# Corner merges of six triangular inverses in seven shared runs, with paired modulation tiles

## The chip, the cores and the metric

The kernel runs on one core of a Trainium2 chip. The metric is the device time of one execution in microseconds (us). TensorE (PE in the profile) has two parts there: PE for the matmuls and PEld for the loads of their stationary operands. VectorE is DVE, ScalarE is ACT, GpSimd is POOL, and SP issues nearly all DMAs from one queue.

## The reference

Two layers of a diffusion backbone run over 128 context tokens and 256 latent tokens, 384 in all, which the kernel handles as three token tiles of 128. A layer computes a modulated RMSNorm, one wide input projection, three mixers (A: windowed attention, B: latent attention, C: a gated delta rule in both directions), a gated merge of the three branches, an output projection and a squared-ReLU MLP. The parts that the change touches are these:

```python
def adaln(cond, w, bias):                       # the modulation vectors
    return (jax.nn.silu(cond) @ w + bias)[:, None, :]
...
    a_mat = jnp.where(strict, jnp.einsum('bhnid,bhnjd->bhnij', kb, kc) * decay, 0.0)
    eye = jnp.eye(C_CHUNK, dtype=f32)
    t_mat = lax.linalg.triangular_solve(eye + a_mat, jnp.broadcast_to(eye, a_mat.shape),
                                        left_side=True, lower=True, unit_diagonal=True)
    u = t_mat @ (vc * bc[..., None])
...
def rmsnorm(x, g):
    xf = x.astype(jnp.float32)
    y = xf * lax.rsqrt(jnp.mean(xf * xf, axis=-1, keepdims=True) + EPS)
    return (y * g.astype(jnp.float32)).astype(x.dtype)
```

The inverse of the unit triangular 128x128 matrix is wanted for 3 token tiles, 2 directions and 4 heads.

## The kernel before, in words

Nearly all of TensorE's work is the dense projections. A weight tile of 128x1024 (512 KB) is loaded into a `raw` buffer (three of them), ACT rounds it into `whi` (L147) and DVE subtracts to get `wlo` (L148), and `mm3` (L151 to L153) forms each product from three matmuls of 384 columns.

Every engine runs its instructions in an order that is fixed when the program is built. Within a phase of a layer a piece of work belongs to a stream, and the order is made by priority: `chain` first, then `fill`. The chain of branch C is a long sequence of small steps; while it waits for DVE or ACT, the matmuls of `merge` (the dense gates and branch projections) and of `beside` fill TensorE.

The inverse is made in two stages. First 32x32 diagonal blocks of all 24 matrices are inverted together on DVE (31 steps, L847 and L849), which gives `Xc` and `XcT` in a packed form. Then, for each of the six pairs of token tile `n` and direction `d`, a loop (L865 to L897) merges blocks: it spreads the packed blocks into full 128x128 tiles `X0` and `X0T` (two DVE products with a block-diagonal mask, L870), cuts the blocks that couple 32-neighbours out of the matrix `M` with `mask5` (`M5`, L865), and then runs five groups of four matmuls (one for each head) with an evacuation between each two: W = M5 X0T (128x128), a product for the transposed 64-block (64 columns of the array), W X0 (128x128), and two 64x64x64 products that fill the last corner. A float32 matmul stands in the profile as two records. ACT evacuates with L878 and L893, DVE with L886, L888 and L897. One merge starts after the other in program order; all matmuls go through the helper `mm` (L156).

`rows` (L188) turns a column of per-token factors into a row repeated on all partitions: three bf16 `pieces` (L177, four DVE instructions) of the factor are each multiplied with an identity, accumulating. It is used for every RMSNorm and for the output gates of branch C.

`ada` (L277) computes modulation rounds 1 and 2 of layer 0: each step loads one 512 KB half tile of `w_ada` and issues four matmuls that write 32 partitions each (groups `g`). `merge(2, more, (1, 1))` calls one step in each of its eight iterations, using the `raw` buffers, and `merge(1, more, (3, 3))` three in each, using three buffers `araw`. `ada_sums` (L294) computes layer 1's modulation on DVE during layer 0's MLP: one step (two DVE instructions, L313) in each of the 32 iterations of the first MLP product, two in each of the 32 of the second, 96 in all.

## Time and profile before

| | |
|---|---|
| median of 3 runs | 1564.96 us (1561.77 to 1565.35) |
| the profiled execution | 1564.52 us, of which 1562.7 us lie between its first and last instruction (the span) |
| busy share of the span | PE 97%, PEld 89%, DVE 65%, ACT 49%, POOL 1% |
| mean granted TensorE clock | 0.993 of full speed |
| DMA | 212.82 MB, 136 GB/s in the mean |

A matmul's recorded duration covers its passage through the array, so two matmuls that follow each other overlap in the record. What one costs is read from the distance between starts. The numbers of layer 0's stages repeat in layer 1 some 779 us later.

### The profile page before, as it was taken

What the parts mean: (1) busy time and instruction counts of PE and PEld (TensorE: products, weight loads), DVE (VectorE), ACT (ScalarE), POOL (GpSimd) and SP (SyncE); (2) the same over time, 40 slices, a digit from 0 to 9 for tenths busy, and PEclk for the clock granted to TensorE, in tenths of its full rate; (3) what the DMA queues carried; (4) which work ended last, traced back from release to release, by engine and by line L of the source; (5) the groups of instructions that cost most, each with busy time, mean ns of one, the idle gap of its engine ahead of it and who ended that gap; (6) DMA issues with size and microseconds to landing.
All of it is one profiled execution on the core that took longest, in us unless ns stands there. A gap on an engine that the chain in (4) does not pass through costs nothing.

```text
span 1562.7 us, 25131 instructions
## 1 busy us (share of the span) xinstructions
PE 1521.6 (97%) x9652; PEld 1396.2 (89%) x9652; DVE 1013.9 (65%) x2187; ACT 771.8 (49%) x1522; POOL 12.9 (1%) x34
## 2 busy tenths in 40 slices
PE   5999999999999999999999999999999999999998
PEld 3898788987888999999988987889888999999997
DVE  4667896475435877789986778955655565553332
ACT  3466633346524666643344676334465446664222
POOL 0000100000000000000000001000000000000000
PEclk9999999999999999999998999999999999999999
DMA  9532131143488555578763331311424434433332
GB/s 315 162 103 88 48 95 48 59 145 105 141 291 279 160 175 176 176 236 259 252 187 98 95 95 47 96 49 58 129 61 135 130 118 126 126 122 129 128 122 81
DMA packets 80857, 212.82 MB, mean 136 GB/s; under 512 B 8801, under 2 KB 24545, under 8 KB 80609
## 3 DMA queue, kind: packets, MB, share of 16 engines
q1 hardware_dynamic: 80736, 211.21, 42.7%
q8 instruction: 76, 1.25, 0.3%
q14 instruction: 45, 0.36, 0.1%
HBM read 204.59 MB, written 4.75 MB: 134 GB/s over the span
## 4 chain that ended last, share of the span: by engine, by line
PE 86%; DVE 8%; DMA 4%; ACT 1%; issue 1%; SPq 0%; DVEq 0%; ACTq 0%
PE g L151 22%; PE g L153 22%; PE g L152 22%; PE c L156 9%; PE f L156 3%; DMA araw<-in_w_ada_dram 2%; PE o L156 2%; PE f L443 2%; DVE wlo L148 2%; PE g L156 1%; DVE h L847 1%; DVE blk L849 1%; DMA mraw<-in_w_ada_dram 1%; PE c L151 1%; PE c L153 1%
## 5 line engine op out<-in xcount | busy, mean ns | idle before, releaser
L147 ACT CAST whi<-raw 128x1024 fp32r<-128x1024 f32 x268 | 280.8, 1048 | 463.6 <-PE g L152 408.0
L153 PE MATMUL g<-hh,wlo 128*128 128x384 f32 (+1 forms) x1440 | 495.2, 345 | 2.8 <-DVE wlo L148 2.7
L151 PE MATMUL g<-hh,whi 128*128 128x384 f32 (+1 forms) x1440 | 494.8, 345 | 3.1 <-ACT hh L229 1.5
L152 PE MATMUL g<-hl,whi 128*128 128x384 f32 (+1 forms) x1440 | 493.6, 344 | 1.3 <-DVE hl L230 1.0
L148 DVE TENSOR_TENSOR wlo<-raw,whi 128x1024 fp32r<-128x1024 f32 x268 | 326.0, 1217 | 168.5 <-PE g L153 123.1
L151 PEld LDWEIGHTS g<-hh,whi 128*128 128x128 f32 x1440 | 272.2, 189 | 14.9 <-issue 6.3
L153 PEld LDWEIGHTS g<-hh,wlo 128*128 128x128 f32 x1440 | 272.5, 189 | 12.4 <-DVE wlo L148 6.0
L152 PEld LDWEIGHTS g<-hl,whi 128*128 128x128 f32 x1440 | 272.2, 189 | 8.1 <-issue 2.7
L151 PE MATMUL g<-fh,whi 128*128 128x384 f32 x512 | 172.9, 338 | 0.0
L152 PE MATMUL g<-fl,whi 128*128 128x384 f32 x512 | 172.1, 336 | 0.0
L153 PE MATMUL g<-fh,wlo 128*128 128x384 f32 x512 | 172.1, 336 | 0.0
L313 DVE SCALAR_TENSOR_TENSOR aacc<-araw,cs,aacc 128x512 f32<-128x512 f32 x168 | 116.5, 747 | 11.0 <-DMA araw<-in_w_ada_dram 6.9
L151 PEld LDWEIGHTS g<-fh,whi 128*128 128x128 f32 x512 | 96.2, 188 | 1.6 <-issue 1.6
L152 PEld LDWEIGHTS g<-fl,whi 128*128 128x128 f32 x512 | 96.3, 188 | 0.0
L153 PEld LDWEIGHTS g<-fh,wlo 128*128 128x128 f32 x512 | 96.3, 188 | 0.0
L156 PE MATMUL c<-g,g 128*128 128x128 f32 (+1 forms) x608 | 77.5, 274 | 3.6 <-DVE g L870 3.1
L156 PEld LDWEIGHTS c<-g,g 128*128 128x128 f32 (+1 forms) x608 | 69.9, 182 | 11.3 <-ACT g L878 4.0
L151 PE MATMUL g<-brh,whi 128*128 128x384 f32 x192 | 66.4, 346 | 0.4 <-ACT whi L147 0.4
L152 PE MATMUL g<-brl,whi 128*128 128x384 f32 x192 | 65.7, 342 | 0.0
L153 PE MATMUL g<-brh,wlo 128*128 128x384 f32 x192 | 65.6, 342 | 0.0
L424 ACT ACTIVATE at_p<-at_p,at_nm 128x384 f32<-128x384 f32 (+1 forms) x96 | 51.8, 541 | 24.7 <-DVE at_nm L421 23.9
L148 DVE TENSOR_TENSOR fl<-fa,fh 128x384 fp32r<-128x384 f32 x64 | 35.6, 556 | 41.9 <-ACT fh L147 41.9
(312 smaller groups left out, 1862.3 us busy)
## 6 DMA issues: line engine op xcount, KB each, us to landing
raw<-in_w_ff_dram SPq DMA_DIRECT2D x128, 512.0 KB, 3.6
raw<-in_w_in_dram SPq DMA_DIRECT2D x102, 512.0 KB, 3.6
araw<-in_w_ada_dram SPq DMA_DIRECT2D x96, 256.0 KB, 3.4
raw<-in_w_branch_dram SPq DMA_DIRECT2D x24, 512.0 KB, 3.6
araw<-in_w_ada_dram SPq DMA_DIRECT2D x24, 512.0 KB, 6.4
raw<-in_w_out_dram SPq DMA_DIRECT2D x16, 512.0 KB, 4.3
mraw<-in_w_ada_dram SPq DMA_DIRECT2D x8, 512.0 KB, 9.2
mraw<-in_w_ada_dram SPq DMA_DIRECT2D x16, 256.0 KB, 7.6
```

The source lines that it names most:

```text
L147: S.copy(hi, src)
L148: V.tensor_tensor(out=lo, in0=src, in1=hi.bitcast(F32), op=ALU.subtract)
L151: PE.matmul(ps, lhsT=wh, rhs=rh, start=start, stop=False)
L152: PE.matmul(ps, lhsT=wh, rhs=rl, start=False, stop=False)
L153: PE.matmul(ps, lhsT=wl, rhs=rh, start=False, stop=stop)
L156: return PE.matmul(ps, lhsT=lhsT, rhs=rhs, start=start, stop=stop)
L313: V.scalar_tensor_tensor(out=acc[:, s, :], in0=raw, scalar=cs[:, k, s:s + 1], in1=acc[:, s, :], op0=ALU.mult, op1=ALU.add)
L424: S.activation(sm[:, :nk], sm[:, :nk], AF.Exp, bias=nm[:, u:u + 1], scale=-1.0, accum_out=den[:, u:u + 1])
L443: PE.transpose(pt[:, j * P:(j + 1) * P], ps_[half, n][:, c * P:(c + 1) * P], ident)
L847: V.tensor_tensor(out=tmp, in0=Cb[:, j + 1:, j:j + 1].to_broadcast([P, r, w]), in1=X[:, j:j + 1, :w].to_broadcast([P, r, w]), op=ALU.mult)
L849: V.tensor_tensor(out=X[:, j + 1:, :w], in0=X[:, j + 1:, :w], in1=tmp, op=ALU.subtract)
```

## The change

The edits are these.

- The six merges are no longer done one after the other. Their products are cut into 64x64x64 pieces, 28 for each (n, d) in place of 20 matmuls, and issued in seven `run`s that mix token tiles and steps. Within a run the pieces alternate between the upper and the lower half of the contraction partitions (`r`), each half with a PSUM bank of its own (`pair`, `twin`). `spread` writes only two 32-blocks per row, so it has 256 columns instead of 512. Evacuations work on 64 partitions. `M5` and the copy `M2` are gone: GpSimd zeroes the 32x32 diagonal blocks of `M` in place instead, and the result is written back into `M`.
- `rows` transposes the float32 column, broadcast to 128 columns, in place of three bf16 matmuls; `pieces` is left for the decay alone.
- A step of `ada` now loads both halves of a tile and issues eight matmuls together, so there are 16 steps: 4 in `merge(2)` and 12 in `merge(1)`, with four `araw` buffers. `ada_sums` has its blocks in another order, and eight of its steps move from the second MLP product into the first.
- `mask5` and the wide block mask go, a sum `bd2` of two mask halves comes (one DVE instruction); pools `g`, `h` and `kq` are resized.

```diff
-    mask5 = [cst[:, C_M5 + d * P:C_M5 + (d + 1) * P] for d in range(2)]
     maskA = [cst[:, C_MA + i * T:C_MA + (i + 1) * T] for i in range(2)]
     cosA, sinA = cst[:, C_RA:C_RA + 256], cst[:, C_RA + 256:C_RA + 512]
     cosB, sinB = cst[:, C_RB:C_RB + 256], cst[:, C_RB + 256:C_RB + 512]
-    bdmask = cst[:, C_BD:C_BD + P]
+    bd2 = mk(cp, [P, 64], "bd2")
...
-    def rows(b, j0, n):
+    def rows(y, j0, n):
 
         ps = bank()
         for j in range(n):
-            for i in range(3):
-                mm(ps[:, j * P:(j + 1) * P], b[i][:, j0 + j:j0 + j + 1].to_broadcast([P, P]), ident16, i == 0, i == 2)
+            PE.transpose(ps[:, j * P:(j + 1) * P], y[:, j0 + j:j0 + j + 1].to_broadcast([P, P]), ident)
         return ps[:, :n * P]
...
-        return rows(pieces(rsqrt(ps[:, 0:3], 3, scale)), 0, 3)
+        return rows(rsqrt(ps[:, 0:3], 3, scale), 0, 3)
...
+                raws = []
                 for half in range(2):
+                    raws.append(mk(ada_pool[0], [P, 1024], ada_pool[1], bufs=ada_pool[2]))
                     c0 = r * 2048 + half * 1024
-                    raw = mk(ada_pool[0], [P, 1024], ada_pool[1], bufs=ada_pool[2])
-                    nc.sync.dma_start(raw, A["w_ada"][l, k * P:(k + 1) * P, c0:c0 + 1024])
-                    rv = raw.rearrange("p (b g i) -> p g b i", b=8, g=4)
+                    nc.sync.dma_start(raws[half], A["w_ada"][l, k * P:(k + 1) * P, c0:c0 + 1024])
+
+                def block(half, g):
+                    rv = raws[half].rearrange("p (b g i) -> p g b i", b=8, g=4)
+                    return mm(ps[32 * g:32 * g + 32, half * 256:half * 256 + 256].rearrange("p (b i) -> p b i", b=8),
+                              cs[:, k, :], rv[:, g], start=k == 0 and half == 1, stop=k == KT - 1 and half == 0)
+
+
+                first = block(1, 0)
+                with tc.issue_after(first.ins):
+                    for g in range(1, 4):
+                        block(1, g)
                     for g in range(4):
-                        mm(ps[32 * g:32 * g + 32, half * 256:half * 256 + 256].rearrange("p (b i) -> p b i", b=8),
-                           cs[:, k, :], rv[:, g], start=k + half == 0, stop=k + half == KT)
-                    if k + half == KT:
-                        modulation(l, r, ps)
-                    yield
+                        block(0, g)
+                if k == KT - 1:
+                    modulation(l, r, ps)
+                yield
...
-                        for s in range(2):
+                        def block(s, g):
                             av = acc[:, s, :].rearrange("p (b g i) -> p g b i", b=4, g=4)
+                            return mm(ps[32 * g:32 * g + 32, q * 128:q * 128 + 128].rearrange("p (b i) -> p b i", b=4),
+                                      pick[:, s, :], av[:, g], start=q == 0 and s == 1, stop=q == 3 and s == 0)
+
+                        first = block(1, 0)
+                        with tc.issue_after(first.ins):
+                            for g in range(1, 4):
+                                block(1, g)
                             for g in range(4):
-                                mm(ps[32 * g:32 * g + 32, q * 128:q * 128 + 128].rearrange("p (b i) -> p b i", b=4),
-                                   pick[:, s, :], av[:, g], start=q + s == 0, stop=q + s == 4)
+                                block(0, g)
...
+            V.tensor_tensor(out=bd2, in0=cst[:, C_BD:C_BD + 64], in1=cst[:, C_BD + 64:C_BD + P], op=ALU.add)
...
-            return mk(ccp, [P, 4, P], "g", bufs=24)
+            return mk(ccp, [P, 4, P], "g", bufs=22)
...
-            return mk(ccp, [P, 4, 64], "h", bufs=3)
+            return mk(ccp, [P, 4, 64], "h", bufs=7)
...
+            for d in range(2):
+                for b in range(4):
+                    G.memset(Mg[n, d][32 * b:32 * b + 32, :, 32 * b:32 * b + 32], 0.0)
...
+        heads = lambda t: t.rearrange("p (h c) -> p h c", h=4)
+        flat2 = lambda t: t.rearrange("p h c -> p (h c)")
+        blocks = lambda t: t.rearrange("p h (b c) -> p h b c", b=2)
+        x0s = [blk().rearrange("p a b -> p (a b)"), mk(ccp, [P, 4, T], "queries", bufs=1).rearrange("p h c -> p (h c)")[:, :1024]]
+        x0s = [t.rearrange("p (i h c) -> p i h c", i=4, h=4) for t in x0s]
+        X0 = {(n, d): x0s[n % 2][:, d] for n in range(3) for d in range(2)}
+        X0T = {(n, d): x0s[n % 2][:, 2 + d] for n in range(3) for d in range(2)}
+        WT, X1T, W2 = {}, {}, {}
+        at = lambda q, h: slice(q * 256 + h * 64, q * 256 + h * 64 + 64)
+        side = lambda q: slice(q * 256, q * 256 + 256)
+
+        def pair():
+            return [bank(), bank()]
+
+        def run(*sets):
+
+            firsts, rest = [], []
+            for makes in sets:
+                lo = [m for r, m in makes if r == 0]
+                hi = [m for r, m in makes if r == 1]
+                order = [m for two in zip(hi, lo) for m in two]
+                firsts += order[:2]
+                rest += order[2:]
+            with ExitStack() as after:
+                for m in firsts:
+                    after.enter_context(tc.issue_after(m().ins))
+                for m in rest:
+                    m()
+
+        def each(items, make):
+            return [(make(it, h)[0], lambda it=it, h=h: make(it, h)[1]()) for h in range(4) for it in items]
+
+        def p1(n, ps):
+            return each([(d, b) for d in range(2) for b in range(2)],
+                        lambda i, h: (i[1], lambda: mm(ps[i[1]][half[i[1]], at(i[0], h)], Mg[n, i[0]][half[i[1]], h, half[i[1]]],
+                                                       X0T[n, i[0]][half[i[1]], h, :])))
+
+        def p2(ns, pt):
+            return each([(n, d) for n in ns for d in range(2)],
+                        lambda i, h: (i[1], lambda: mm(pt[i[1]][half[i[1]], at(i[0] % 2, h)], X0[i][half[i[1]], h, :],
+                                                       WT[i][half[i[1]], h, :])))
+
+        def p3(n, ps):
+            return each([(d, b) for d in range(2) for b in range(2)],
+                        lambda i, h: (i[1], lambda: mm(ps[i[1]][half[i[1]], at(i[0], h)], WT[n, i[0]][half[i[1]], h, :],
+                                                       X0[n, i[0]][half[i[1]], h, :])))
+
+        def p4(ns, pt):
+            return each([(n, d) for n in ns for d in range(2)],
+                        lambda i, h: (i[1], lambda: mm(pt[i[1]][half[1 - i[1]], at(i[0] % 2, h)],
+                                                       Mg[i][half[i[1]], h, half[1 - i[1]]], X1T[i][half[i[1]], h, :])))
+
+        def p5(ns, pt):
+            return each([(n, d) for n in ns for d in range(2)],
+                        lambda i, h: (1 - i[1], lambda: mm(pt[1 - i[1]][half[i[1]], at(i[0] % 2, h)], W2[i][half[1 - i[1]], h, :],
+                                                           Mg[i][half[1 - i[1]], h, half[1 - i[1]]])))
+
+        def spread(n):
             for d in range(2):
                 u0 = (2 * n + d) * 4
-                hs, os = half[d], half[1 - d]
-                M = Mg[n, d]
-                M5 = g4()
-                V.tensor_tensor(out=M5, in0=M, in1=mask5[d].unsqueeze(1).to_broadcast([P, 4, P]), op=ALU.mult)
-                M2 = h4()
-                V.tensor_copy(M2[hs], M[hs, :, os])
-                X0, X0T = M, g4()
-                for dst, c in ((X0T, (Xc, XcT)[d]), (X0, (XcT, Xc)[d])):
-                    V.tensor_tensor(out=dst.rearrange("p h (b c) -> p h b c", b=4),
-                                    in0=c[:, u0:u0 + 4, :].unsqueeze(2).to_broadcast([P, 4, 4, 32]),
-                                    in1=bdmask.rearrange("p (b c) -> p b c", b=4).unsqueeze(1).to_broadcast([P, 4, 4, 32]),
+                for dst, c in ((X0T[n, d], (Xc, XcT)[d]), (X0[n, d], (XcT, Xc)[d])):
+                    V.tensor_tensor(out=blocks(dst), in0=c[:, u0:u0 + 4, :].unsqueeze(2).to_broadcast([P, 4, 2, 32]),
+                                    in1=bd2.rearrange("p (b c) -> p b c", b=2).unsqueeze(1).to_broadcast([P, 4, 2, 32]),
                                     op=ALU.mult)
-                ps = bank()
-                for h in range(4):
-                    mm(ps[:, h * P:(h + 1) * P], M5[:, h, :], X0T[:, h, :])
-                WT = g4()
-                S.copy(flat(WT), ps)
-                pt = bank()
-                for h in range(4):
-                    mm(pt[hs, h * 64:h * 64 + 64], X0[:, h, hs], WT[:, h, hs])
-                ps = bank()
-                for h in range(4):
-                    mm(ps[:, h * P:(h + 1) * P], WT[:, h, :], X0[:, h, :])
-                X1T = h4()
-                V.tensor_tensor(out=X1T[hs], in0=X0T[hs, :, hs], in1=pt[hs, 0:256].rearrange("p (h c) -> p h c", h=4),
-                                op=ALU.subtract)
-                V.tensor_tensor(out=flat(X0), in0=flat(X0), in1=ps, op=ALU.subtract)
-                ps = bank()
-                for h in range(4):
-                    mm(ps[os, h * 64:h * 64 + 64], M2[hs, h, :], X1T[hs, h, :])
-                W2 = h4()
-                S.copy(W2[os].rearrange("p h c -> p (h c)"), ps[os, 0:256])
-                ps = bank()
-                for h in range(4):
-                    mm(ps[hs, h * 64:h * 64 + 64], W2[os, h, :], X0[os, h, os])
-                V.tensor_scalar(out=X0[hs, :, os], in0=ps[hs, 0:256].rearrange("p (h c) -> p h c", h=4), scalar1=-1.0,
+
+        def e1(n, ps):
+            for d in range(2):
+                WT[n, d] = h4()
+                for b, hs in enumerate(half):
+                    (S.copy if b else V.tensor_copy)(flat2(WT[n, d][hs]), ps[b][hs, side(d)])
+
+        def e2(n, pt):
+            for d in range(2):
+                X1T[n, d] = h4()
+                V.tensor_tensor(out=X1T[n, d][half[d]], in0=X0T[n, d][half[d]], in1=heads(pt[d][half[d], side(n % 2)]), op=ALU.subtract)
+
+        def e3(n, ps):
+            for d in range(2):
+                for b, hs in enumerate(half):
+                    V.tensor_tensor(out=Mg[n, d][hs, :, hs], in0=X0[n, d][hs], in1=heads(ps[b][hs, side(d)]), op=ALU.subtract)
+
+        def e4(n, pt):
+            for d in range(2):
+                W2[n, d] = h4()
+                S.copy(flat2(W2[n, d][half[1 - d]]), pt[d][half[1 - d], side(n % 2)])
+
+        def e5(n, pt):
+            for d in range(2):
+                V.tensor_scalar(out=Mg[n, d][half[d], :, half[1 - d]], in0=heads(pt[1 - d][half[d], side(n % 2)]), scalar1=-1.0,
                                 scalar2=None, op0=ALU.mult)
-                Xi[n, d] = X0
+                Xi[n, d] = Mg[n, d]
+
+        spread(0)
+        spread(1)
+        t1, t2 = twin(), pair()
+        run(p1(0, t1), p1(1, t2))
+        e1(0, t1)
+        e1(1, t2)
+        t1, t2 = twin(), pair()
+        run(p3(0, t2), p2((0, 1), t1))
+        e2(0, t1)
+        e2(1, t1)
+        e3(0, t2)
+        spread(2)
+        t1, t2 = twin(), pair()
+        run(p3(1, t2), p4((0, 1), t1))
+        e4(0, t1)
+        e4(1, t1)
+        e3(1, t2)
+        t1, t2 = twin(), pair()
+        run(p1(2, t2), p5((0, 1), t1))
+        e5(0, t1)
+        e5(1, t1)
+        e1(2, t2)
+        t1, t2 = twin(), pair()
+        run(p3(2, t2), p2((2,), t1))
+        e2(2, t1)
+        e3(2, t2)
+        t1 = twin()
+        run(p4((2,), t1))
+        e4(2, t1)
+        t1 = twin()
+        run(p5((2,), t1))
+        e5(2, t1)
...
-        r = pieces(r)
...
-        merge(2, more, (1, 1))
+        merge(2, more, (1, 0))
         es.close()
         ab.close()
         with tc.tile_pool(name=f"ada{l}", bufs=1, reuse_waits="tile") as pool:
-            ada_pool[:] = pool, "araw", 3
-            merge(1, more, (3, 3))
+            ada_pool[:] = pool, "araw", 4
+            merge(1, more, (1, 2))
...
-            next(more, None)
+            for _ in range(2 if t % 4 == 3 else 1):
+                next(more, None)
```

`tc.issue_after` adds an ordering on the same engine without a semaphore: what is issued inside comes behind the named instruction.

## Rows read from the trace of the kernel before

**Rows 1.** The page: busy time of each engine, its share, instructions.
```profile
PE 1521.6 (97%) x9652; PEld 1396.2 (89%) x9652; DVE 1013.9 (65%) x2187; ACT 771.8 (49%) x1522; POOL 12.9 (1%) x34
```

**Rows 2.** Windows: busy time (instructions) of PE, PEld, DVE, ACT, POOL; granted clock.
```profile
1400.00:1500.00 100.00, 100.00 (x577) 100.00 (x576) 38.87 (x50) 35.68 (x48) 0.00 (x0) 1.00 0.38 128
226.30:264.88 38.58, 36.65 (x305) 30.79 (x303) 31.08 (x46) 9.64 (x17) 0.00 (x0) 1.00 0.15 48
802.00:826.00 24.00, 21.05 (x127) 16.39 (x125) 19.32 (x60) 12.03 (x24) 0.00 (x0) 0.94 0.36 108
```

**Rows 3.** The window of layer 0's merges, instructions of line 156 alone: PE, PEld.
```profile
226.30:264.88 38.58, 24.91 (x240) 21.44 (x240) 1.00 0.15 48
```

**Rows 4.** Timeline of PE, first merge: start, duration, operation, count [idle <- releaser].
```profile
228.24 1.16 PE L156 MATMUL c<-g,g 128*128 128x128 f32 x8 [1.57 <-DVE g L870]
229.15 0.42 PE L153 MATMUL g<-hh,wlo 128*128 128x384 f32 x1
...
231.77 0.68 PE L156 MATMUL c<-h,h 64*64 64x64 f32 x8
232.37 0.44 PE L151 MATMUL g<-hh,whi 128*128 128x384 f32 x1
232.65 0.34 PE L152 MATMUL g<-hl,whi 128*128 128x384 f32 x1
```

**Rows 5.** Chain that ended last, scores of branches A and B: start, us, what.
```profile
80.56 0.85 PE f L156 x4
...
353.10 1.29 PE f L156 x4
```

**Rows 6.** Timeline of PE, attention output of branch A.
```profile
111.22 1.30 PE L156 MATMUL o<-at_pT,vA 128*64 128x128 f32 x12
112.35 0.60 PE L156 MATMUL o<-at_pT,vAc 128*64 128x256 f32 x4
112.88 0.38 PE L156 MATMUL f<-kA,qA 64*128 64x128 f32 x2
```

**Rows 7.** Groups by line and form, DVE: busy, mean ns | idle before.
```profile
L870 DVE TENSOR_TENSOR g<-blk,cst 128x512 f32<-128x512 f32 x24 | 24.7, 1045 | 0.5
L886 DVE TENSOR_TENSOR h<-g,c 64x256 f32<-64x256 f32 x12 | 5.0, 417 | 3.1 <-PE c L156 3.0
L313 DVE SCALAR_TENSOR_TENSOR aacc<-araw,cs,aacc 128x512 f32<-128x512 f32 x168 | 116.5, 747 | 11.0 <-DMA araw<-in_w_ada_dram 6.9 <-ACT aacc L311 4.0
L148 DVE TENSOR_TENSOR wlo<-raw,whi 128x1024 fp32r<-128x1024 f32 x267 | 325.5, 1219 | 168.5 <-PE g L153 123.1 <-issue 22.9 <-ACT g L954 19.8
```

**Rows 8.** Timeline of PE: a run of `rows`, and four transposes of branch B.
```profile
308.54 0.84 PE L156 MATMUL c<-ident,piece 128*128 128x128 bf16 x12
309.19 0.42 PE L153 MATMUL g<-hh,wlo 128*128 128x384 f32 x1
...
417.55 0.66 PE L443 MATMUL f<-cst,at_p 128*128 128x128 f32 x4
417.96 0.42 PE L152 MATMUL g<-hl,whi 128*128 128x384 f32 x1
```

**Rows 9.** Timeline of DVE at the start of layer 1.
```profile
809.87 0.17 DVE L182 CAST piece<-rs_y 128x3 bf16<-128x3 f32 x1
...
813.30 0.35 DVE L227 SCALAR_TENSOR_TENSOR tmp<-x,gp,c 128x128 f32<-128x128 f32 x1 [0.79 <-PE c L156]
```

**Rows 10.** Timeline of PE: a single modulation step, and three in one run.
```profile
424.00 0.64 PE L156 MATMUL g<-raw,cs 128*32 128x256 f32 x8
424.57 0.44 PE L151 MATMUL g<-hh,whi 128*128 128x384 f32 x1
...
447.20 1.50 PE L156 MATMUL g<-araw,cs 128*32 128x256 f32 x24
448.63 0.44 PE L151 MATMUL g<-hh,whi 128*128 128x384 f32 x1
```

**Rows 11.** Windows: `merge(1)` of layer 0, first MLP product; last: DMA share, GB/s.
```profile
431.00:497.00 66.00, 64.40 (x484) 55.32 (x484) 29.45 (x46) 20.85 (x29) 0.00 (x0) 1.00 0.86 288
540.00:664.00 124.00, 124.00 (x740) 122.63 (x739) 94.43 (x160) 85.60 (x154) 0.00 (x0) 1.00 0.55 171
```

3 lines of the change are left out of this document (1 added, 2 removed).

## The prediction

> **What bounds the kernel now.** I read the page first: TensorE is busy for 97% of the span, DVE for 65%, ACT for 49% [rows 1]. The reader should not take the 97% as work that cannot shrink, because a matmul's record overlaps the next one. The second view, windows over quiet stages, gives the real price: in the second MLP product of layer 1 577 records of 384 columns fill 100 us, so one costs 0.173 us [rows 2]. TensorE's order is fixed, and while the chain of branch C waits, dense fill is put in between; the fill must be done anyway. So time that the chain takes from TensorE lengthens the kernel, and time that is taken from the chain's waits alone does not.
>
> The third view is the window of layer 0's six merges. It lasts 38.58 us and holds 305 matmul records [rows 2], of which 240 are the merges' own [rows 3]; the other 65 are fill and are worth 65 x 0.173 = 11.2 us. The merges thus take 38.6 - 11.2 = 27.4 us of TensorE's time in each layer. The fourth view, the timeline, shows what this is made of [rows 4]. At the start TensorE waits for the spread on DVE: 1.57 us of idle time. Eight records of 128 columns then occupy 0.91 us (228.24 to 229.15), 0.114 each. Eight records of 64x64x64 occupy 0.60 us (231.77 to 232.37). Half of 0.114 is 0.057, so 0.46 of the 0.60 is their rate and 0.14 is paid once per run; the fill after it loses another 0.1 (0.28 between its first two starts in place of 0.173), and I take 0.1 on entry: about 0.34 us for every visit of the chain.
>
> **The merges, part by part.** After the change a layer has 28 pieces for each of six pairs, 168 matmuls or 336 records of 64 columns, in seven runs of 32, 32, 32, 32, 24, 8 and 8 matmuls. If nothing overlapped, they would take 336 x 0.057 = 19.2 us, as much as before. The question is whether two pieces in opposite halves of the array run together. The trace shows each half of that. Two heads on different contraction rows: four records of 384 columns take 0.85 us on 64-row operands, and 1.29 us where the operands are 96 rows high [rows 5]. Two heads on different output columns: 16 records, four of 128 and twelve of 256 columns, take 112.88 - 111.22 = 1.66 us [rows 6]; one after the other, at 1.29 / 4 / 384 = 0.84 ns per column from rows 5, they would take 3.0 us. So both kinds of pairs overlap almost wholly, and the new order alternates them as these do. No row has pieces that differ in rows and in columns at once, and none so short. I take full overlap: 9.6 us. Both ends stay: 9.6 and 19.2.
>
> The Trainium skill, page TensorEngine Tiling (Array Packing), section Key Properties, says that different tiles load and multiply in parallel, and that a change of the tiling mode drains the array. By it the sum would be the 9.6 us that I take; the drain would be part of the 0.34 us per visit.
>
> Seven visits cost 7 x 0.34 = 2.4 us. The wait ahead of the first run stays and should grow: it now needs eight spread instructions in place of two. Each is half as wide, so I estimate 1.045 / 2 = 0.52 us [rows 7], 4.2 us in place of 2.1. DVE is already late there by 1.6 us; the order knows of the six more instructions and can put fill there, so I add only an estimated 0.1 for each, 2.2 us, and for the later runs 6 x 0.2 us. What is late next is the first weight subtraction (`wlo`, 1.22 us, rows 7) queued behind the spread on DVE; its two buffers cover it. Evacuations of 64x256 cost 0.42 us [rows 7]; between the second and third run eight of them stand on DVE, 3.3 us, and the order can put 19 fill records there. DVE's total falls, since the full-width spread and the mask product go; it has 31.1 of 38.6 us now [rows 2].
>
> After: 9.6 + 2.4 + 2.2 + 1.2 = 15.4 us. Gain per layer 27.4 - 15.4 = 12.0, both layers 24 us. Bounds: without overlap 27.4 - 25.0 = 2.4 per layer, 5 us; with overlap and no wait but the 0.34s 27.4 - 12.0 = 15.4, 30 us.
>
> GpSimd's 48 zeroings cost nothing: POOL is busy 1% [rows 1] and they precede the 31 DVE steps. Should they delay these, the fill that runs meanwhile covers it; without that cover it would be their own time, 24 small instructions in a layer.
>
> **The row broadcasts.** 144 bf16 records become 48 transposes. Twelve records occupy 0.65 us, and four transposes 0.41 us [rows 8], so a token tile falls from 0.163 to 0.103: 48 x 0.06 = 2.9 us. I take 3, for the pieces arrive one by one and split runs today; bounds 1 and 5. At the start of layer 1 the four DVE instructions stand on the path: from the first cast to the first instruction that uses the row 3.43 us pass [rows 9], with a weight subtraction queued in between. Three transposes and a semaphore need about 0.7 us, so some 2.7 us go where TensorE waits for the modulated inputs (granted clock 0.94, DVE 19.3 of 24 us, rows 2). Moving the last eight modulation steps out of this corner frees DVE a little more. I take 3, bounds 1 and 4. Elsewhere the pieces are hidden by fill, the final ones of branch C too; if that fill were gone they would cost the same 2.7 us each.
>
> **The modulation.** A lone step of eight records takes 0.57 us, and three in one run 1.43 us [rows 10]: 0.43 per step and 0.14 per run, to which I add 0.2 for entry and the fill after it. In `merge(2)` eight runs at 0.77 become four of 16 records at 1.2: 6.2 - 4.8 = 1.4 us. In `merge(1)` there are eight runs before and after, 24 steps in all, so nothing. That stage moves 288 GB/s at a DMA share of 0.86 [rows 11], so it cannot become much shorter; a fourth buffer may remove some of its waits. I take 2, bounds 0 and 5.
>
> **MLP.** Eight steps more in the first product add 8 x 2 x 0.747 = 12 us of DVE [rows 7] to 32 iterations; the share there is 94.4 of 124 us, 76% [rows 11], and becomes about 85%. An iteration with two steps is longer than TensorE's, the next three make it good. Cost 0, at worst 2. `bd2` and pool sizes: nothing; DVE meets `bd2` at the start of layer 0's chain, behind a load that it waits for there anyhow.
>
> **Sum.** 24 + 3 + 3 + 2 = 32 us. The profiled execution took 1564.5 us (span 1562.7), close to the median of 1564.96; 1564.5 - 32 = 1532.5, say 1532.
>
> **Rivals.**
> *The pieces do not overlap* (records of 64 columns are too short to gain, or both kinds of tiling at once exclude each other). For it: no row shows this shape paired. Against: rows 5 and 6. The merges then give 5 and not 24: 1564.5 - 13 = 1551.
> The page just named warns under Instruction Overhead not to tile a dimension that is small, as each matmul has a fixed cost; by it the time would lie near this rival's, while the trace has 64-column records at half the price of 128.
>
> *The runs wait on each other.* All pieces of a step now end together, so the evacuations come in a lump: 4, 8, 4, 6 and 6 instructions of 0.42 us stand on DVE behind the first five runs, 11.8 us a layer. If the fixed order puts no fill there, the merges keep nearly nothing: 24 less 2 x (11.8 - 1.2) leaves 3, and with the other 8 us the time is 1553. Against: today's order puts four to six fill records into each gap.
>
> *Slower: the clock falls in the merges.* The granted clock is 1.00 in this stage now, and 0.94 around 815 us, where TensorE waits for DVE in short pieces [rows 2]. If the new runs leave such holes and the clock goes from 2.4 to 1.2 GHz for the stage, 27 us of TensorE work per layer (12 of pieces, 15 of fill) take twice as long: 1532 + 54 = 1586. It decides from 16 us of work per layer at the low level on, which gives the 32 us back. For: idle time is concentrated. Against: the 1.57 us wait of today leaves the clock at 1.00.
>
> **How the numbers follow.** Forecast 0.66, with its own range 1518 to 1546; no overlap 0.13; waiting runs 0.09; clock 0.05; something unlisted, half of it within 0.3% and half slower, 0.07. The lower end takes all upper bounds, 30 + 5 + 4 + 5 = 44: 1520, and a little more for waits that may go unseen: 1516. The upper end holds the first rival and most of the second: 1555. Within 0.3% (4.7 us, about what a measurement of this kernel can tell from no change) lie a part of the waiting runs, 0.03, and half of the unlisted: 0.06. Slower: 0.05 + 0.03 = 0.08. Faster: the rest, 0.86.
>
> **What would show it.** Right: 336 records of 64x64 in each layer's merges, two starts a few ns apart and about 0.057 us from such a pair to the next; a run of 32 matmuls within 2.2 us; TensorE's idle time ahead of the first run near 2.2 us; 48 transposes in place of 144 bf16 records; the merge stage's window, less its fill, at about 15 us. Wrong: every start 0.057 us behind the last; idle time released by DVE or ACT evacuations of more than 1 us between the runs; a granted clock below 1 there; araw waits of several us in `merge(2)`, whose pairs hold two of three `raw` buffers.

## The result, and the profile after

The changed kernel takes 1539.63 us (median of 4 runs, 1535.33 to 1540.17), the kernel before 1563.53 us beside it: ratio 0.9841, 95% interval 0.9818 to 0.9864. That is a gain of 24 us where 32 were forecast; the time lies inside the range. The profiled execution took 1539.34 us (span 1537.5), 25.2 less than the one of before, and the stages below account for that.

The page of the changed kernel, busy time of each engine; it answers to [rows 1].

```profile
PE 1495.3 (97%) x9748; PEld 1381.0 (90%) x9748; DVE 993.8 (65%) x2148; ACT 768.0 (50%) x1522; POOL 22.4 (1%) x82
```

TensorE has 96 records more and is busy for 26 us less. To find where, both spans are cut at the same instructions: the first broadcast matmul of `bar` in branch C's chain, ahead of the merges, the last of its `oss` sums (its end), the first 386-column record of each MLP.

| stage, us | before | after | difference | forecast |
|---|---|---|---|---|
| up to the chain of layer 0 | 158.99 | 158.51 | -0.5 | 0 |
| chain of layer 0, with its merges | 143.32 | 130.46 | -12.9 | -12 |
| from there to the MLP (rows, modulation) | 221.51 | 218.68 | -2.8 | -3.5 |
| MLP of layer 0 | 280.11 | 281.73 | +1.6 | 0 |
| start of layer 1, up to its chain | 135.09 | 135.12 | 0.0 | -3 |
| chain of layer 1, with its merges | 141.70 | 129.05 | -12.7 | -12 |
| from there to the MLP (rows) | 198.52 | 198.81 | +0.3 | -1.5 |
| MLP of layer 1 and the end | 283.49 | 285.11 | +1.6 | 0 |

(The forecast's 3 us for the rows outside the start of layer 1 stand half in each layer.) The second and third line need a correction, for dense work moved from the one stage into the other. Windows of the line of the hi-times-hi matmuls alone show it (PE busy and records, PEld, clock, DMA); first the kernel before, then the changed one, the chain of layer 0 and the stage behind it:

```profile
158.99:302.31 143.32, 43.33 (x122) 23.46 (x122) 0.99 0.20 60
302.31:523.82 221.51, 103.60 (x298) 56.02 (x298) 1.00 0.58 189
```

```profile
158.51:288.97 130.46, 41.39 (x117) 22.49 (x117) 0.97 0.23 68
288.97:507.65 218.68, 105.04 (x303) 56.96 (x303) 1.00 0.58 191
```

Five such matmuls, 15 records with their partners, 15 x 0.173 = 2.6 us, are now done behind the chain (in layer 1 as well). The chain itself gained 12.9 - 2.6 = 10.3 us in layer 0 and 12.7 - 2.6 = 10.1 in layer 1; the stages behind it gained 5.4 and 2.3.

Windows of the changed kernel, all engines, in the columns of [rows 2]: the merges of layer 0, their first run, the first MLP product, and the start of layer 1.

```profile
225.60:253.10 27.50, 25.09 (x396) 21.32 (x395) 22.57 (x46) 8.94 (x20) 0.00 (x0) 0.94 0.16 46
...
228.40:231.80 3.40, 3.40 (x58) 3.19 (x57) 3.18 (x8) 0.37 (x1) 0.00 (x0) 0.52 0.02 5
...
540.00:664.00 124.00, 124.00 (x764) 121.72 (x763) 108.10 (x180) 81.12 (x144) 0.00 (x0) 1.00 0.65 200
...
789.40:801.40 12.00, 11.16 (x69) 9.38 (x67) 9.23 (x31) 7.09 (x14) 0.00 (x0) 1.00 0.41 124
801.40:807.40 6.00, 0.35 (x1) 0.29 (x1) 5.90 (x18) 4.15 (x11) 0.00 (x0) 0.83 0.01 1
807.40:813.40 6.00, 6.00 (x19) 5.03 (x19) 5.42 (x18) 3.04 (x9) 0.00 (x0) 0.50 0.58 173
813.40:819.40 6.00, 6.00 (x30) 6.00 (x29) 3.75 (x14) 1.75 (x4) 0.00 (x0) 0.81 0.11 20
```

Two places stand out by their clock: the first run of the merges (0.52) and the start of layer 1, where TensorE does nothing for six microseconds and then works at half speed. The timeline of PE shows the runs (answers to [rows 4]):

```profile
227.54 0.33 PE L155 MATMUL f<-blk,g 64*64 64x64 f32 x4 [1.60 <-DVE blk L940]
...
228.46 1.73 PE L155 MATMUL f<-blk,g 64*64 64x64 f32 x28
230.06 1.76 PE L155 MATMUL c<-queries,g 64*64 64x64 f32 x28
231.75 0.53 PE L151 MATMUL g<-hl,whi 128*128 128x384 f32 x1
...
238.96 0.27 PE L155 MATMUL c<-queries,h 64*64 64x64 f32 x1
238.96 0.27 PE L155 MATMUL f<-h,g 64*64 64x64 f32 x2
...
240.67 0.44 PE L152 MATMUL g<-hh,wlo 128*128 128x384 f32 x1
241.48 0.33 PE L150 MATMUL g<-hh,whi 128*128 128x384 f32 x1
242.57 0.29 PE L155 MATMUL c<-blk,g 64*64 64x64 f32 x2 [0.77 <-DVE g L958]
...
800.04 0.34 PE L150 MATMUL g<-hh,whi 128*128 128x384 f32 x1
800.22 0.34 PE L151 MATMUL g<-hl,whi 128*128 128x384 f32 x1
807.05 1.06 PE L150 MATMUL g<-hh,whi 128*128 128x384 f32 x2 [6.49 <-ACT kab L498]
```

In the first run 56 records take 231.75 - 228.46 = 3.29 us, 0.059 each, at the low clock. In the third 64 records take 240.67 - 238.96 = 1.71 us, 0.027 each, and two of them start within the same 10 ns: the pieces do overlap. At 800.22 TensorE stops until the copy `kab` has emptied an accumulator.

### The profile page after: what moved, and what is told of

It is laid out like the page before. It is cut to its first block, busy times and chain, and to the rows that moved or that the text cites. A ratio compares the mean times of both kernels' runs of the same rounds, so it can differ in the third digit from the quotient of the medians.

```text
span 1537.5 us, 25331 instructions
## 1 busy us (share of the span) xinstructions
PE 1495.3 (97%) x9748; PEld 1381.0 (90%) x9748; DVE 993.8 (65%) x2148; ACT 768.0 (50%) x1522; POOL 22.4 (1%) x82
## 5 line engine op out<-in xcount | busy, mean ns | idle before, releaser
L349 DVE SCALAR_TENSOR_TENSOR x<-g,mod,x 128x128 f32<-128x128 f32 x64 | 23.7, 412 | 52.4 <-PE g L152 48.7
L1227 ACT ACTIVATE fa<-fa,fb 128x128 f32<-128x128 f32 (+1 forms) x128 | 51.1, 446 | 0.7 <-DVE fa L1225 0.7
```

Of the source, the lines that this page charges most:

```text
L349: V.scalar_tensor_tensor(out=x[k][:, c], in0=ps[:, c], scalar=m[:, b0 + k, s:s + 1], in1=x[k][:, c], op0=ALU.mult, op1=ALU.add)
L1227: S.activation(a[:, c], a[:, c], AF.Relu, bias=b[:, s:s + 1])
```

## The experiments

The eleven runs were compared with the kernel before, on the same chip. All start from the changed kernel.

**e1, unpaired pieces.**

```
-                rest += order[2:]
+                rest += hi[1:] + lo[1:]
```

> The changed kernel (1539.6 us) with one edit: inside each shared run the pieces on rows 64 to 127 are issued first and then those on rows 0 to 63 (the first two of each set stay as they were), so that neighbours no longer lie in opposite halves of the array. Everything else is as changed. Theory 'pairs overlap because neighbours use different rows and different columns': with the order gone, most of the 336 records of a layer follow each other at 0.057 us, runs 2 to 7 lose up to 9 us in each layer, and the time is 1550 to 1558 us. Rival 'the gain came from the shared evacuations and fewer visits of the chain, and records of 64 columns would run at 0.029 us in any order': within 3 us of 1539.6.

Measured: 1559.34 us (1551.21 to 1572.17), ratio 0.9977, interval 0.9950 to 1.0004: the whole gain is gone. More is lost than the theory's 10 to 18 us, and the windows of the merges of both layers say why:

```profile
224.40:271.20 46.80, 45.17 (x400) 39.19 (x398) 21.38 (x45) 8.83 (x24) 0.00 (x0) 0.60 0.09 27
...
1009.00:1043.00 34.00, 32.38 (x400) 28.03 (x400) 21.65 (x46) 9.01 (x25) 0.00 (x0) 0.90 0.12 37
```

In layer 0 nearly the whole stage ran at the low clock. Layer 1 is the fair comparison: 34.00 us at 0.90, where the changed kernel has 28.00 (990 to 1018 us, 399 records, 0.94). By these means of full and half clock e1 is at half for 3.4 us longer (34.00 x 0.10 x 2 less 28.00 x 0.06 x 2), which costs 1.7; it also has eight fill records fewer there, 1.4 us. The two nearly cancel. Its timeline holds a stretch in which all neighbours lie in one half:

```profile
1022.39 0.28 PE L155 MATMUL f<-h,queries 64*64 64x64 f32 x2
1022.50 0.28 PE L155 MATMUL f<-h,blk 64*64 64x64 f32 x2
1022.62 0.28 PE L155 MATMUL f<-h,queries 64*64 64x64 f32 x2
1022.74 0.28 PE L155 MATMUL f<-h,blk 64*64 64x64 f32 x2
1022.85 0.28 PE L155 MATMUL f<-h,queries 64*64 64x64 f32 x2
```

Eight records start in 1022.85 - 1022.39 = 0.46 us, 0.058 each, against 0.027 in pairs. So the order of the pieces is worth 6 us a layer at a like clock, although e1 leaves some pairs; it would be 0.031 x 336 = 10.4 if every record lost its partner. The rival falls, but not the whole of what it names: a layer's chain gained 10 us, and some 4 of them are left without the order. Fewer visits, the narrower spread and the shared evacuations can have brought these; no run takes them apart. The rest of the 20 us goes with the clock: over e1's ten executions the time falls from 1572.17 us at a mean granted clock of 0.970 to 1551.21 at 0.986, and all ten lie below the changed kernel's 0.991.

**e2, X0T first.**

```
-        spread(0)
-        spread(1)
+        spread(0, (0,))
+        spread(1, (0,))
         t1, t2 = twin(), pair()
         run(p1(0, t1), p1(1, t2))
+        spread(0, (1,))
+        spread(1, (1,))
```

(`spread` takes a second argument that selects the X0T, the X0 products or both.)

> The changed kernel with one edit: of the eight spread instructions ahead of the first run only the four that write X0T, which the first run reads, come before it; the four that write X0 come behind it. Theory 'the first run is late and at half clock because it waits for eight spreads': TensorE is idle some 2 us less ahead of the first run, the run's 64 records take 1.9 us in place of 3.3 at a granted clock near 1, and each layer gains 2 to 3.5 us: 1532.5 to 1536 us. Rival 'the wait only moves on': the second run needs X0 and waits for the other four spreads and the evacuations behind them, and the time stays within 1.5 us of 1539.6. Second rival: the wait is shorter, but the clock in the first run is low all the same, since idle time before it remains: 1537 to 1538 us.

Measured: 1535.70 us, ratio 0.9827 (0.9812 to 0.9841). The first run took place at full clock, its last 56 records in 1.8 us, in both layers, and from the first piece to the last e2 took 24.0 us in each layer, where the changed kernel took 25.4. But TensorE's idle time ahead of the first run is what it was, 1.6 us. From the chain's start to the last piece both layers took 93.1 us, where the changed kernel took 94.4 and 93.0: in layer 1 the part ahead of the merges, which the edit leaves alone, was 1.5 us longer here. Runs e8 and e10 below have the same edit; in e10 the two layers of one execution differ (windows of the first 4 us of the merges, layer 0 and layer 1):

```profile
225.70:229.70 4.00, 4.00 (x72) 3.38 (x72) 4.00 (x9) 0.72 (x3) 0.00 (x0) 1.00 0.00 0
980.84:984.84 4.00, 4.00 (x66) 3.63 (x67) 4.00 (x10) 0.74 (x3) 0.00 (x0) 0.66 0.00 0
```

The code is the same and the wait ahead is the same; from the first piece to the last layer 0 took 24.08 us and layer 1 25.31. Over the eleven profiles that have this wait of 1.6 us, the clock fell in 15 of 22 merge stages: in 3 of the 8 that have the edit (e2, e8, e9, e10), and in 12 of the 14 that have not (in all but those of e5). So the edit did not cure it, and the low clock, worth 1.2 us here, comes and goes; whether the edit makes it rarer, so few stages, two to an execution, cannot tell. My first theory falls, since the wait it wanted to shorten stayed. Of the 4 us by which e2 is faster at most 1.4 a layer lie in the merges, and none can be put down to its edit with certainty.

**e3, padding.**

```
     bd2 = mk(cp, [P, 64], "bd2")
+    mk(cp, [P, 32], "pad")
```

> The changed kernel with 128 bytes per partition of padding in the pool of constants, so that the tiles fh and fl, the moving operands of the second MLP product, lie again at the addresses of the kernel before (they had moved by 128 bytes); no instruction changes. Theory 'the second product lost 2 to 3 us because of the addresses of its moving operands': a record of 384 columns costs 0.173 us again in place of 0.176, the second product is 2.0 us shorter in layer 1 and about 1 us or more in layer 0, and the time is about 1536 to 1537 us. Rival 'the addresses of the weights, or the neighbouring work on DVE and the queues, cost it': 0.176 us stays, and the time is 1539.6 within 1 us.

Measured: 1537.91 us (0.9829 to 0.9864). In layer 1 a record still costs 0.1767 us. The theory of the addresses falls in the form in which I stated it.

**e4, a sweep of addresses.** In layer 1 the `fh` and `fl` tiles are taken from four named groups of eight each, with a tile of 8 floats between the groups.

```
+            for name in ("fh", "fl"):
+                for j, c in enumerate("abcd"):
+                    both += [mk(fp, [P, T], name + c, F32R, bufs=8) for _ in range(8)]
+                    mk(fp, [P, 8], f"pad{name}{c}")
```

> The changed kernel, in which in layer 1 alone the 32 tiles fh and the 32 tiles fl lie in four groups of eight each, with 32 bytes of padding between the groups: the eight groups start at 32, 64, 96, 128 (fh), 160, 192, 224 and 0 (fl) bytes past a multiple of 256. Each output tile of the second MLP product passes through the four groups in turn, 24 records each. Theory 'address': the four stretches of an output tile run at rates that differ by 1 to 3 per cent, in the same order for all eight output tiles, those of groups near 96 slow and near 224 or 0 fast. Rival: all four take the same time within 0.3 per cent.

Measured: 1536.61 us in one run. The timeline of one output tile, at the first record of each group and of the next tile:

```profile
1422.13 0.34 PE L150 MATMUL g<-fha,whi 128*128 128x384 f32 x1
...
1426.35 0.34 PE L150 MATMUL g<-fhb,whi 128*128 128x384 f32 x1
...
1430.58 0.34 PE L150 MATMUL g<-fhc,whi 128*128 128x384 f32 x1
...
1434.75 0.34 PE L150 MATMUL g<-fhd,whi 128*128 128x384 f32 x1
...
1438.93 0.34 PE L150 MATMUL g<-fha,whi 128*128 128x384 f32 x1
```

The four stretches of 24 records take 4.22, 4.23, 4.17 and 4.18 us, 0.174 to 0.176 each, and so in all eight output tiles. The rival, all four within 0.3 per cent, falls: the pace changes at the groups, with no other matmul in between, and in the same way in every tile. Placement does matter by up to 1.5 per cent, but not as I thought: the group at 96, which the theory had among the slow ones, is the fastest here.

**e5, early copy.** The two early projections are copied to `kab` and `sqacc` ahead of `modulated`:

```
+                held.append((t, b, M))
+            hh, hl = modulated(rb, gp1, mod0, 0)
+            for t, b, M in held:
                 V.tensor_tensor(out=t, in0=t, in1=rb[:M], op=ALU.mult)
```

> The changed kernel (1539.6 us) with one edit at the start of layer 1: the two early projections are copied out of their accumulators (to kab and sqacc) ahead of the modulated inputs, and only scaled and shifted behind them. Theory 'the 3 us of the row broadcasts were lost there because TensorE stands for 6.8 us, from 800.2 to 807.0 in the changed kernel, until an accumulator is free that stands behind all the modulated inputs': the accumulators come free earlier, the idle stretch shrinks to about 2 to 4 us, the granted clock behind it stays higher, and the time falls by 2.5 to 5 us, to 1534.5 to 1537. Rival 'TensorE would only wait for the modulated inputs themselves': the same time passes until the first records of 128x384 run one behind the other, and 1539.6 changes by less than 1 us.

Measured: 1532.99 us (ratio 0.9817, 0.9786 to 0.9848). The start of layer 1 takes 130.6 us in place of 135.1, 4.5 us less; the theory gave 2.5 to 5 for the whole time, which is 6.6 us shorter. Both merge stages ran at full clock here, from the first piece to the last in 24.6 us. TensorE is still idle for 3.3 us at the start of layer 1, in place of 6.5.

**e6, old modulation,** and **e7, old row broadcasts:** the lines of the kernel before for `ada`, `ada_sums` and their calls in e6, and for `rows` and its callers in e7.

> The changed kernel with the modulation as in the kernel before: single tiles of eight records, steps (1, 1) and (3, 3), three buffers, one step in each iteration of the first MLP product. Theory (the forecast's term): 2 us of the gain were the modulation's, so 1541 to 1542 us; the stage of the two merges behind branch B is 1.5 to 3 us longer. Rival: the pairs gain nothing, since this stage is bound by its transfers: 1539.6 within 1 us, and the eight steps given back to the second MLP product show as up to 1 us on either side.

> The changed kernel with the row broadcasts as in the kernel before: three bf16 pieces and three matmuls for each row (the pieces in one small buffer each). Theory (the forecast's two terms, with what the trace showed of them): 3 us come back in the chain's end and in branch B's inputs, nothing at the start of layer 1, where the stall for an accumulator hides the pieces: 1542 to 1543 us. Rival 'the forecast was right for the start of layer 1 as well, and the stall there came with the order of the modulation steps': 1545 to 1546 us. Third: the pieces were hidden all along: within 1 us of 1539.6.

Measured: e6 1535.43 us (0.9804 to 0.9849), e7 1541.09 (0.9838 to 0.9885). Stage by stage, us:

| | before | after | e6 | e7 |
|---|---|---|---|---|
| behind the chain of layer 0 | 221.5 | 218.7 | 222.0 | 222.1 |
| behind the chain of layer 1 | 198.5 | 198.8 | 198.7 | 201.1 |
| start of layer 1 | 135.1 | 135.1 | 127.4 | 126.6 |

In their totals neither run came out as its theory or its rivals had it; the stages say why. Two things at once. The modulation is worth 222.0 - 218.7 = 3.3 us and the rows 3.4 + 2.3 = 5.7 where they were meant to act, both more than forecast. And each of the two edits alone has a start of layer 1 that is 8 us shorter than that of the kernel before and of the changed kernel. No theory that I had put on record said that; e7's rival laid the stall to the order of the modulation steps, but e7 keeps those steps and does not stall. The order of TensorE's instructions in the programs explains it. In the changed kernel two matmuls of the first full projection are followed by one of a second and two of a third, whose accumulators the two early projections still hold; there TensorE stops, with work of the first at hand. In e6 and e7 six matmuls of the first come before the second is opened, and the third is opened later still.

**e8, one more matmul,** on top of e2:

```
+            if l and d:
+                mm(ps[:, 0:1], ident, ones1)
```

> The kernel with the X0T spreads first (1535.7 us), and in layer 1 one more matmul of one column ahead of each but the first output tile of the second MLP product; its result is not used. It moves everything behind it by one place in TensorE's stream of instructions, eight different places in one run. In this product a record cost 0.1767 us in all kernels so far that have the change, 0.1733 in the kernel before and in layer 0 of all, with the moving tiles at the same addresses too. Theory 'it depends on where the loop lies in TensorE's stream of instructions': some of the eight output tiles run at 0.1733 and some at 0.1767 us a record. Rival 'it depends on addresses of data or on other engines': all eight stay at 0.1767. The time differs by less than 3 us either way.

Measured: 1538.21 us in one run. Windows of the first three output tiles of layer 1, each from the start of one record to the start of the 90th after it:

```profile
1388.62:1404.52 15.90, 15.90 (x92) 15.90 (x91) 5.65 (x6) 5.45 (x8) 0.00 (x0) 1.00 0.39 119
1405.80:1421.52 15.72, 15.72 (x92) 15.72 (x92) 5.00 (x5) 3.92 (x5) 0.00 (x0) 1.00 0.37 120
1422.80:1438.70 15.90, 15.90 (x91) 15.90 (x91) 5.46 (x6) 3.91 (x5) 0.00 (x0) 1.00 0.40 120
```

0.1767, 0.1747, 0.1767 us a record, and so on in turn: each inserted matmul flips the pace, and it holds for the whole tile. The pace of 0.1733 that the theory named does not occur.

**e9, late steps,** on top of e2:

```
-            for _ in range(2 if t % 4 == 3 else 1):
-                next(more, None)
+            next(more, None)
```

> The kernel with the X0T spreads first (1535.7 us) with one more edit: the first MLP product runs one modulation step in each iteration, as the kernel before, so that the last eight steps stand in the second product again; the paired tiles and the steps (1, 0) and (1, 2) stay. In TensorE's order the first projection of layer 1 then takes six matmuls before the order opens the next accumulator, in place of two, as in the runs with the old modulation and with the old row broadcasts. Theory 'the start of layer 1 lost its 3 us, and 8 us in all against what it can be, because the order opens a third accumulator after three matmuls and TensorE stands behind it': the stage from the end of the second product to the first full projection of layer 1 takes 127 us in place of 135, the granted clock stays at 1 in it, and the time is 1526.5 to 1529 us. Rival 'what helped in those two runs was that DVE had other work there': the stall comes back in another place, 1533 to 1536 us.

Measured: 1531.03 us, ratio 0.9784 (0.9766 to 0.9801). The start of layer 1 takes 127.4 us, as said; windows of it (compare the last four of the changed kernel above):

```profile
786.84:798.84 12.00, 12.00 (x87) 10.34 (x87) 9.70 (x31) 5.86 (x11) 0.00 (x0) 1.00 0.56 170
798.84:804.84 6.00, 5.09 (x27) 4.50 (x27) 5.46 (x16) 3.88 (x10) 0.00 (x0) 1.00 0.43 130
804.84:810.84 6.00, 5.27 (x29) 4.44 (x29) 5.84 (x13) 4.58 (x10) 0.00 (x0) 1.00 0.24 55
810.84:816.84 6.00, 6.00 (x37) 5.87 (x35) 4.77 (x19) 4.14 (x12) 0.00 (x0) 1.00 0.67 203
```

DVE is nearly as busy as there (5.5 and 5.8 of 6), TensorE is idle 1.6 us in place of 6.5, and the clock stays at 1. The rival (DVE's other work helped) falls: the stall did not come back. That it is the order in which accumulators are opened is read from the programs and from the 6.49 us wait for `kab`; e5, which empties the accumulators earlier and leaves DVE its work, speaks for it with its 3.3 us. The whole is 2 us above the upper end of what I expected; both merge stages had the low clock in this execution.

**e10, other extras,** on top of e9: the matmul of e8 replaced by one of another kind for each output tile.

> The kernel of the run with the late steps, and in layer 1 other small matmuls ahead of the second to the eighth output tile of the second MLP product, of a different kind each time (their results are not used): one of one column in bf16, one of 128 columns, two of one column, four of 128 columns on 32 output rows, one of 384 columns, one of 64, two of 128 in bf16. Theory 'the pace of this product is set by what came before it in TensorE's stream and then lasts until the next disturbance': within each output tile the pace is the same from record to record, it changes only at the inserted matmuls, and lies between 0.1733 and 0.1767 us. Rival 'the pace belongs to the data's addresses in layer 1': 0.1767 us whatever is inserted.

Measured: 1530.44 us in one run. The eight tiles run at 0.1767, 0.1767, 0.1747, 0.1747, 0.1767, 0.1733, 0.1747 and 0.1747 us; the sixth, behind a matmul of 384 columns, is the one at 0.1733 (window as above):

```profile
1466.20:1481.80 15.60, 15.60 (x91) 15.60 (x91) 5.06 (x5) 3.50 (x4) 0.00 (x0) 1.00 0.40 119
```

Within this run the theory holds: the pace changes at the inserted matmuls alone, and not at each of them. The rival falls. But e4 had the pace change with nothing inserted, so what came before is not all that sets it.

**e11, a later first run,** on top of e9:

```
-        run(p1(0, t1), p1(1, t2))
+        with tc.issue_after(projected[-5].ins):
+            run(p1(0, t1), p1(1, t2))
...
+            if l and d == 1:
+                mm(ps[:, 0:T], ident, x[0])
```

> The kernel of the run with the late steps (1531.0 us) with two more edits. First, the first run of the merges is ordered on TensorE behind the end of the dense projection that it cut at its fifteenth record, ten records (1.7 us) later; the work is the same. Second, in layer 1 one matmul of 384 columns, whose result is not used, stands ahead of the second output tile of the second MLP product. Theory for the first, 'the idle 1.6 us ahead of the first run are there because the order puts it too early, and the half clock in the first two runs follows from the idle time': TensorE is no longer idle ahead of the first run, the granted clock is 1 through the merges, the stretch from the first bf16 broadcasts of the chain to the last piece takes 90 to 91.5 us in place of 92.9 and 94.4 in the two layers. Rival: the idle time is only moved behind the first run, where the ten records are missing, and the stretch keeps its length. Theory for the second, 'the pace is set by what came before': the first output tile runs at 0.1767 us a record, the other seven at 0.1733, and the product is 1.6 us shorter. Together 1525 to 1528 us; with both rivals 1531.

Measured: 1531.55 us (0.9773 to 0.9816), the same as e9. Windows: the 2 us ahead of the first run, the run, and the 6 us behind it; the last row is layer 1:

```profile
226.05:228.05 2.00, 2.00 (x12) 1.75 (x11) 2.00 (x4) 0.10 (x1) 0.00 (x0) 1.00 0.17 66
228.05:230.05 2.00, 2.00 (x62) 1.88 (x63) 2.00 (x5) 1.34 (x2) 0.00 (x0) 1.00 0.00 0
230.05:232.05 2.00, 1.69 (x17) 1.30 (x13) 2.00 (x4) 0.00 (x0) 0.00 (x0) 1.00 0.00 0
232.05:236.05 4.00, 2.14 (x44) 1.82 (x45) 1.94 (x5) 1.22 (x4) 0.00 (x0) 1.00 0.45 131
989.23:993.23 4.00, 2.12 (x13) 1.56 (x15) 1.96 (x5) 1.22 (x4) 0.00 (x0) 0.68 0.43 135
```

The wait ahead is gone and the clock is 1, as the theory said; but the wait is back behind the run, 1.9 us of 4, and in layer 1 the clock falls there. The stretch from the chain's start to the last piece takes 94.7 and 96.8 us. Nine dense records more than in e9 stand in it, 9 x 0.173 = 1.6 us; without them it is 93.1 and 95.2 us, not shorter than e9's 92.9 and 94.4: the rival was right. Of the second edit, the first tile ran at 0.1767 and the seven others at 0.1747, not the 0.1733 that the same matmul gave in e10. That the pace changes there was right; its value was not foreseen. The best version that ran is therefore e9, faster than both kernels.

## Why the prediction was right or wrong

**The merges: mechanism right, size 20 us, not 24.** Two pieces that differ in rows and columns run together, as [rows 5] and [rows 6] suggested apart (0.85 us against 1.29 there, and 1.66 against 3.0; "almost wholly" was more than the first shows). e1 takes the pairs away, and 6 of the 10 us a layer go; the other 4 were not taken apart. The Trainium skill, TensorEngine Tiling (Array Packing), section Key Properties, says that different tiles execute in parallel; the runs agree, 0.027 us a record in pairs and 0.058 alone; in the changed kernel's trace many starts come in twos, 7 ns apart and 59 ns from two to two, the sign that the forecast named. Its warning under Instruction Overhead did not apply to pieces of this size here: they still gained. By the forecast's own sum a layer's merges should take 15.4 us. The window from 225.60 holds 396 records, of which 51 are fill and 9 belong to the next step; with [rows 4]'s 0.114 for each of the nine it gives 27.5 - 51 x 0.173 - 9 x 0.114 = 17.7 us. 0.8 to 1.2 of the missing 2.3 us are the low clock in the first run (25.35 us from the first piece to the last in layer 0, 24.58 in e5 at full clock; e10's two layers); the rest I did not settle. The wait ahead of the first run, 2.2 us in the forecast, measured 1.60; the largest later one is 0.77, on the DVE evacuation.

**The clock rival came in part.** I gave 0.05 to a clock that falls in the merges, and took the 1.57 us wait of before, which left it at 1.00, as evidence against. That step failed: a wait as long, 1.60 us, is followed by half clock in 15 of 22 merge stages. Its price was 1.2 us between the two layers of e10, and 13 us between those of e1 (44.65 us from the first piece to the last in layer 0, 31.64 in layer 1), where it stayed low through a whole stage. The Trainium skill, TensorE: Matmul & The Clock Gate, section HAM oscillation, describes waits in a kernel's loop that throw the clock back to half. The rows agree for the wait at the start of layer 1, 6.49 us with 0.50 behind it. The 1.60 us ahead of the merges are shorter than the waits of that section, and are followed by 0.52 in most stages and by 1.00 in others; there the measurement decides.

**Rows: 5.7 us where 3 were forecast, modulation 3.3 where 2 were.** Both were under-sized, the rows by 0.7 beyond their upper bound of 5; 48 transposes (line 191) replace the 144 records as said. The two do not simply add: against the kernel before, the stages behind the chains gained 5.4 + 2.3 = 7.7 us.

**The start of layer 1: the step that failed.** "I take 3", for the pieces that stand on DVE's path ahead of the modulated inputs. The pieces went, and DVE's first modulated product began 6.5 us after the second product's end in place of 9.4. In the kernel before TensorE did wait there for the modulated inputs, 2.5 us in six waits, and 1.1 for `kab`; the last three of the seven:

```profile
822.76 0.44 PE L151 MATMUL g<-hh,whi 128*128 128x384 f32 x1 [0.57 <-ACT hh L229]
823.53 0.69 PE L152 MATMUL g<-hl,whi 128*128 128x384 f32 x1 [0.33 <-DVE hl L230]
826.62 0.34 PE L576 MATMUL c<-cst,kab 48*128 48x48 f32 x1 [1.12 <-ACT kab L487]
```

In the changed kernel these waits are gone, and one of 6.49 us for an accumulator, at a point that TensorE's fixed order sets, stands in their place (the row at 807.05 above). The forecast took the inputs for the only thing that TensorE would wait for there, and that failed. I had also cut [rows 2]'s window at 826 us and read a clock of 0.94; windows that run past it show that the kernel before had half clock behind its waits as well:

```profile
821.90:827.90 6.00, 3.98 (x12) 2.41 (x11) 5.58 (x12) 3.88 (x9) 0.00 (x0) 0.61 0.01 3
827.90:833.90 6.00, 6.00 (x21) 5.91 (x22) 3.64 (x18) 1.60 (x6) 0.00 (x0) 0.54 0.58 186
```

e9 shows the price, 7 us against e2 (127.4 in place of 134.6) and 8 against the changed kernel: there the eight modulation steps stand in the second product again. I had read their move as relief for DVE, "a little more". They are not the cause by themselves: e7 has them moved and does not stall, and the kernel before has them where they were, waits for its inputs, and takes 135.1 us. With the new rows and the new steps together the planned order stalls; with either alone (e6, e7, e9) it does not. Why the order comes out so is not shown.

**MLP: forecast 0, at worst 2; measured 3.2.** The first product of layer 0 lost 0.75 us with DVE at 108.1 of 124 us, 87% where 85 were forecast: that part is right. The second product lost 0.9 us in layer 0 and 2.6 in layer 1 (the rest of that layer's MLP and the end give 1.0 back), and in layer 1 no work there had changed. In layer 0 a wait of 0.36 us for `wlo` at 768.24 and the last output tile, at 0.1767 us a record, make up most of the 0.9. Windows of 90 record intervals in the same output tile, of before and then of after:

```profile
1467.64:1483.24 15.60, 15.60 (x92) 15.60 (x91) 5.70 (x7) 4.14 (x5) 0.00 (x0) 1.00 0.38 124
```

```profile
1441.36:1457.26 15.90, 15.90 (x92) 15.90 (x92) 5.69 (x7) 4.13 (x5) 0.00 (x0) 1.00 0.39 118
```

This is the pace of e8 and e10. It was not in the forecast and could not have been read from the rows of before. What fixes it stays open: not the addresses alone (e3, e4), and not DVE, ACT or the queues, which come and go in these windows while it stays.

The sum: 20.4 + 7.7 + 0 - 3.2, and 0.5 ahead of the first chain, makes 25.4; the span is 25.2 shorter, the rest is rounding.

## What to carry to other kernels

Order small matmuls so that neighbours differ in rows and in columns: 0.058 us a record becomes 0.027. Where a planner fixes TensorE's order, a small edit far away can cost more than the one that is studied: cut the span into stages at the same instructions, try each part of a change without the others, and look at which accumulator the order opens before its last reader is done. Price a wait by the stage's end, not by its own length: moved away in one place (e11), it came back behind.

## What the runs showed that I had not expected

A long run of 384-column matmuls settles at one of a few paces, 0.1733, 0.1747 or 0.1767 us a record at a granted clock of 1.00, and where its operands lie in one group of tiles it keeps the pace until something comes between; one matmul of one column flips it (e8). With operands in four groups the pace changes from group to group (e4). Over a product of 768 records the ends differ by 2.6 us.

Behind the same wait of 1.6 us the merges ran at full clock in 7 stages and began at half in 15, and once the same code did so differently in the two layers of one execution (e10): a difference of 1 to 2 us between two versions of this kernel is not evidence of an edit, even in a single stage's rows.
